# A slot more for streamed expert weights, and another order of the first expert group

## The chip, the cores and the metric

The kernel runs on 1 core of one Trainium2 chip. A time is the device time of one execution in microseconds (us). Before the change the median of 3 runs is 1218.99 us (1218.17 to 1219.28).

## The reference, cut to what matters

One decoder layer on 256 tokens of width 1024, all in float32. First a token mixer (modulated RMSNorm, one combined projection, gated linear attention and a short convolution, output projection), then a mixture of experts with 64 experts in 8 groups, of which each token uses 2:

```python
x = x + g1[:, None] * y                                   # after the mixer
h = rmsnorm(x, norm2_g[l]) * (1.0 + sc2[:, None]) + sh2[:, None]
p_group = softmax(t @ rg_w + rg_b); g_w, g_idx = top_k(p_group, 1)
e_w, e_loc = top_k(softmax(e_logits[of that group]), 2)   # weights then scaled by g_w
yb = (silu(xblk @ w1[e]) * (xblk @ w3[e])) @ w2[e]        # per expert, 1024 -> 512 -> 1024
x = x + g2[:, None] * y                                   # y: weighted sum of a token's two experts
out = rmsnorm(x, final_norm_g)
```

Every expert's w1, w3 and w2 (6 MB) is read once: 64 experts are 403 MB of the 476 MB that the kernel reads.

## The kernel before

**Stages.** The mixer runs over 88 blocks of projection weights (512 KB each, numbered 0 to 87; the last eight, 80 to 87, are the output projection `O0`, `O1`). TensorE works block after block, each in three passes with a weight split into a high and a low part (ACT line 320, DVE line 327). Then comes the router, then the experts in 16 groups of 4 (`EPG`). An expert group has room for 32 tokens of each of its experts (`CAP`), and 12 units of weights of 2 MB each: units 0 to 7 (`KT`) hold w1 and w3 by rows of the model width, units 8 to 11 hold w2. A token beyond an expert's 32 goes to overflow blocks, worked under a runtime condition before group 13 (`OVG`).

**A group's work.** `slots` writes on DVE the one-hot matrices `P1` and their sum `Pm` (which token goes where), `gather` multiplies the normalized residual with `Pm` on TensorE (line 994) and modulates the result into `xg` on ACT and DVE (lines 998, 1000), `slot_weights` scales `P1` by the router's weights (DVE, lines 1009, 1010) and transposes it on TensorE (line 1014). `l1_unit` multiplies with a unit of w1, w3 (line 1022), `act` does silu and product and transposes, `l2_unit` multiplies with w2, `evac_y` applies the gate, and `combine` brings the rows back to their tokens (line 1049) and adds them to the residual `acc` (line 1050). Within group g, `combine(g - 1)` comes after unit 2 and the inputs of group g + 1 after unit 4. In group 0 it is otherwise: its own gather stands between units 0 to 3, after unit 3 `after_start` (the router's weights and then the overflow tables, DVE lines 949 to 972), after unit 5 `after_start2` (`slot_weights(0)`, and the gate's row `g2r`, line 1075), after unit 6 the inputs of group 1.

**The stream of weights.** All loads of weights are issued by SyncE (SP) in program order, whenever the buffer of an earlier block or unit has been used: `Stream.bfree` (line 58, and line 66 where the blocks have run out) for a quarter of the ring, `Stream.free` (line 87) for a whole slot. There are ten slots of 2 MB: the ring of 12 blocks becomes three of them, the tiles T10, T11, T3, T9, T7, T6 and T4 of the mixer become the other seven, each when its last reader is done. So group 0's units 0 to 9 lie in T10, ring, T11, ring, T3, ring, T9, T7, T6, T4. Units 10 and up follow into whichever slot comes free; nothing but free buffers and the order of the program times them.

**Buffers that the change touches.** `xt` (tile T5) has four quarters of 4 KB per partition: 0 and 1 hold the transposed residual `xres`, later the two gather buffers `xg`; 2 and 3 are scratch of the mixer and then of the router (`r8`), later `y` and `g2r`. Tile T8 holds in turn several arrays of the mixer, at last `sg`, read by the evacuation of block 79; from `o_setup` (called ahead of block 82) it is `wk`: half 0 is the residual `acc`, half 1 its normalized copy `h2`, made by ACT at line 894 and read by every gather.

```python
S.activation(h2[:, tt], acc[:, tt], AF.Copy, scale=rs[:, tt:tt + 1])
...
            if u == (4 if g else 6) and g + 1 < NGRP and g + 1 != OVG:
```

Of the kernel before, what the change touches and what calls it, by code (L numbers as in the profile page):

```python
# [12 lines left out]
AF = mybir.ActivationFunctionType  # L13
# [6 lines left out]
TT = 2  # L20
# [20 lines left out]
CB, CN1, CN2, CGG, CCW, CGB, NCOL = 0, 48, 56, 64, 72, 96, 100  # L41


class Stream:


# [25 lines left out]
        self.bfree(self.at.pop(key))  # L72

    def slot(self, tag):
        if isinstance(tag, int):
            return self.ring[:, 4 * tag:4 * tag + 4].rearrange("p a b -> p (a b)")
        return self.pool.tile([128, 4096], F32, name="unit", tag=tag)

    def free(self, tag):
        if self.n == len(self.units):  # L80
            return
        key, pieces = self.units[self.n]
        self.n += 1
        t = self.slot(tag)
        self.tiles[key], self.tags[key] = t, tag
        for dst, src in pieces:
            self.nc.sync.dma_start(dst(t), src)

    def done(self, key, keep=False):
        tag = self.tags.pop(key)  # L90
        del self.tiles[key]
        if not keep:
            self.free(tag)
        return tag

# [2 lines left out]
def trunk_kernel(ctx: ExitStack, tc: tile.TileContext, xT: bass.AP, c: bass.AP, modw: bass.AP,  # L98
# [536 lines left out]
    B2 = modc[:, 24:32]  # L635
    rconst = sm.tile([128, 72], F32, name="rconst")
    ssq = sm.tile([128, TT, 5], F32, name="ssq")
    r8 = xt[:, 2:4].rearrange("p a b -> p (a b)")

    def pre_router():  # L640
        V.scalar_tensor_tensor(A2, modc[:, 32:40], 1.0, colt[:, CN2:CN2 + 8], op0=OP.add, op1=OP.mult)
# [133 lines left out]

    def o_setup():
        wk = big.tile([128, 2, TT, D], F32, name="wk", tag="T8")
        L["acc"], L["h2"] = wk[:, 0], wk[:, 1]
        L["pl"] = mt(2, 128)
        mring.remove((rot["m"] - 1) % 4)  # L780
        rot["m"] = 0
# [52 lines left out]
    evac(nb, *pend)  # L834
    run(nb)
    run(nb + 1)
    acc, h2 = L["acc"], L["h2"]
    assert not todo

    rs = sm.tile([128, 4], F32, name="rs")  # L840
# [6 lines left out]
    def scratch(*shape):  # L847
        n = 1
        for d in shape:
            n *= d  # L850
        t = r8[:, o[0]:o[0] + n]
        o[0] += n
        assert o[0] <= 2048
        if len(shape) == 2:
            t = t.rearrange("p (a b) -> p a b", a=shape[0])
        return t
# [4 lines left out]
    em, ei = scratch(2, 8), scratch(2, 8).bitcast(U32)  # L861
    OO = sm.tile([128, 2, 2, 64], BF, name="OO")
    O1, O2 = OO[:, :, 0], OO[:, :, 1]
    prr = scratch(4, 64).rearrange("p (t k) e -> p t k e", t=2)
    pr = prr.rearrange("p t k e -> p (t k e)")[:, 0:128].rearrange("p (t e) -> p t e", t=2)
    big8 = scratch(2, 2)
    nm, ex, zz, pw = scratch(2, 2), scratch(64), scratch(2, 2), scratch(2, 2)
# [23 lines left out]
    for tt in range(TT):  # L891
        V.max_index(gi[:, tt], gm[:, tt], lg[:, tt, :8])
    for tt in range(TT):
        S.activation(h2[:, tt], acc[:, tt], AF.Copy, scale=rs[:, tt:tt + 1])
    V.tensor_tensor(off8, io[:, None, :8].to_broadcast([128, 2, 8]), gi[:, :, 0:1].to_broadcast([128, 2, 8]),
                    op=OP.not_equal)
    V.scalar_tensor_tensor(lm.rearrange("p t (g e) -> p t g e", g=8), off8[:, :, :, None].to_broadcast([128, 2, 8, 8]),
# [50 lines left out]
    def overflow_tables():  # L948
        V.tensor_scalar(xb, cnt, float(CAP), None, op0=OP.is_gt)
        for m in range(2, 8):  # L950
            V.scalar_tensor_tensor(xb, cnt, float(CAP * m), xb, op0=OP.is_gt, op1=OP.add)
        V.tensor_tensor_scan(incl, onesf[:, :64], xb, 0.0, op0=OP.mult, op1=OP.add)
        V.tensor_sub(excl, incl, xb)
        for k, ot in enumerate((O1, O2)):
            for tt in range(TT):
                V.scalar_tensor_tensor(pr[:, tt], excl, 1.0, ot[:, tt], op0=OP.mult, op1=OP.mult,
                                       accum_out=ovs[:, tt, k:k + 1])
        V.scalar_tensor_tensor(dov, ovs, float(CAP), rank, op0=OP.mult, op1=OP.add)
        V.tensor_scalar(big8, rank, float(CAP), 8192.0, op0=OP.is_lt, op1=OP.mult)
        V.scalar_tensor_tensor(dov, dov, -float(CAP), big8, op0=OP.add, op1=OP.add)  # L960
        V.tensor_sub(dgo, dov.rearrange("p t k -> p (t k)")[:, :, None].to_broadcast([128, 4, 4]),
                     iog[:, None, 0:4].to_broadcast([128, 4, 4]))
        cmp = gt2[:, 0:NOV * 64].rearrange("p (b e) -> p b e", b=NOV)
        V.tensor_tensor(cmp, incl[:, None, :].to_broadcast([128, NOV, 64]),
                        io[:, :NOV, None].to_broadcast([128, NOV, 64]), op=OP.is_le)
        V.memset(ebi, 0)
        ef = fl(pr)[:, 0:NOV]
        V.tensor_reduce(ef, cmp, axis=AX.X, op=OP.add)
        V.tensor_scalar(ebi[:, 0, :NOV], ef, float(NE - 1), None, op0=OP.min)
        V.tensor_scalar(ebi[:, 1, :NOV], ebi[:, 0, :NOV], 2, None, op0=OP.arith_shift_right)  # L970
        V.tensor_scalar(ebi[:, 2, :NOV], ebi[:, 0, :NOV], 3, None, op0=OP.bitwise_and)
        V.tensor_copy(ebi[:, 0, 15:16], incl[:, 63:64])
# [12 lines left out]
    def gather_part(xg, i, split=False):  # L985
        if split:
            ps = [mt(128) for _ in range(2)]
        else:
            both = mt(2, 128)
            ps = [both[:, j] for j in range(2)]  # L990
        for j in range(2):
            for tt in range(TT):
                f = 256 * i + 128 * j
                T.matmul(ps[j], h2[:, tt, f:f + 128], Pm[:, tt], start=(tt == 0), stop=(tt == 1))  # L994
        for j in range(2):
            k = 2 * i + j
            if i % 2 == 0:
                S.activation(xg[:, k], ps[j], AF.Identity, bias=B2[:, k:k + 1], scale=A2[:, k:k + 1])  # L998
            else:
                V.tensor_scalar(xg[:, k], ps[j], A2[:, k:k + 1], B2[:, k:k + 1], op0=OP.mult, op1=OP.add)  # L1000
# [41 lines left out]
    def combine(key, c0=0, c1=D):  # L1042
        pwt = X["w", key]
        for c in range(c0, c1, 512):
            w = min(512, c1 - c)
            s = slice(c, c + w)
            for tt in range(TT):
                ps = mt()
                T.matmul(ps[:, :w], pwt[:, tt], X["y"][:, s], start=True, stop=True)  # L1049
                V.tensor_add(acc[:, tt, s], acc[:, tt, s], ps[:, :w])  # L1050

    V.tensor_tensor(Pm.rearrange("p t (j s) -> p t j s", j=EPG), pc[:, 0:2, 0:EPG, None].to_broadcast([128, TT, EPG, CAP]),
                    iof[:, None, None, :].to_broadcast([128, TT, EPG, CAP]), op=OP.is_equal)
# [5 lines left out]
    def after_start():  # L1059
        V.tensor_sub(dg, dst.rearrange("p t k -> p (t k)")[:, :, None].to_broadcast([128, 4, NGRP]),  # L1060
                     iog[:, None, 0:NGRP].to_broadcast([128, 4, NGRP]))
        for k in range(2):
            for tt in range(TT):
                V.tensor_scalar(P1[:, k, tt], io, dst[:, tt, k:k + 1], None, op0=OP.is_equal)
        weights()
        overflow_tables()
        S.activation(dum, epsc, AF.Silu)

    def after_start2():
        slot_weights(0)  # L1070
        for hh in range(2):
            p = mt(4, 128)
            for k in range(4):
# [36 lines left out]
                    combine("o")  # L1110

    OVG = NGRP - 3
    fgr = h2[:, 0]
    sq = h2[:, 1]

    def final_gain():
        for hh in range(2):
            p = mt()
            T.matmul(p, onesf[0:1, :], sq[0:1, 512 * hh:512 * hh + 512], start=True, stop=True)
            S.copy(fgr[:, 512 * hh:512 * hh + 512], p)  # L1120

    for g in range(NGRP):
        if g == OVG:
            combine(g - 1)
            held = st.done(("e", g - 1, NU - 1), keep=True)
            overflow(held)
            slots(g, dg, g)
            gather(g, g)
            slot_weights(g)
            st.free(held)  # L1130
        ps = pa.tile([128, D], F32, name="a")
        for u in range(KT):
            if g == 0 and u < 4:
                gather_part(X[0], u, u == 0)
            if g == last and u == 0:
                S.dma_start(sq[0:1, :], bass.AP(tensor=fg.tensor, offset=fg.offset, ap=[[D, 1], [1, D]]))
            if g == last and u == 5:
                final_gain()
# [1 line left out]
            st.done(("e", g, u))  # L1140
            if g == 0 and u == 3:
                after_start()
            if g == 0 and u == 5:
                after_start2()
            if u == 2 and g > 0 and g != OVG:
                combine(g - 1)
            if u == (4 if g else 6) and g + 1 < NGRP and g + 1 != OVG:
                slots(g + 1, dg, g + 1)
                gather(g + 1, g + 1)
                slot_weights(g + 1)  # L1150
        act(ps)
        ps = pa.tile([128, D], F32, name="a")
        if g < last:
            for f in range(4):
                l2_unit(ps, f, unit("e", g, KT + f))
                if not (g + 1 == OVG and f == 3):
                    st.done(("e", g, KT + f))
            evac_y(ps)
    S.activation(dum, epsc, AF.Sqrt)

# [6 lines left out]
    def last_part(n, tail=False):  # L1167
# [2 lines left out]
        evac_y(ps, c0, c0 + cw)  # L1170
        combine(last, c0, c0 + cw)
        for tt in range(TT):
            a = acc[:, tt, c0:c0 + cw]
            if tail and tt == 1:
                V.scalar_tensor_tensor(sq[:, c0:c0 + cw], a, 1.0, a, op0=OP.mult, op1=OP.mult,
                                       accum_out=ssq[:, tt, n:n + 1])
# [2 lines left out]

    def last_weigh(n):  # L1180
        c0, cw = LASTC[n]
        V.tensor_mul(acc[:, :, c0:c0 + cw], acc[:, :, c0:c0 + cw], fgr[:, None, c0:c0 + cw].to_broadcast([128, TT, cw]))  # L1182

    for u in range(2):
        w = st.tiles["e", last, KT + u].rearrange("p (f j c) -> p f j c", f=2, j=EPG)
# [21 lines left out]
    last_weigh(3)  # L1207
    V.reciprocal(rs[:, 0:2], rs[:, 0:2])
    lo, hi = slice(0, 512), slice(512, D)
    V.tensor_scalar(acc[:, 0, lo], acc[:, 0, lo], rs[:, 0:1], None, op0=OP.mult)  # L1210
    nc.sync.dma_start(out[0:128, lo], acc[:, 0, lo])
    S.activation(acc[:, 1, lo], acc[:, 1, lo], AF.Copy, scale=rs[:, 1:2])
    S.dma_start(out[128:256, lo], acc[:, 1, lo])
    for tt in range(TT):
        V.tensor_scalar(acc[:, tt, hi], acc[:, tt, hi], rs[:, tt:tt + 1], None, op0=OP.mult)
        nc.sync.dma_start(out[128 * tt:128 * tt + 128, hi], acc[:, tt, hi])


_INS = ["xT", "c", "modw", "cols", "win", "wgd", "gw2", "wr", "rb", "fg", "ew", "el"]
# [65 lines left out]
```

## Time and profile before

| what | value |
|---|---|
| median of 3 runs | 1218.99 us |
| the profiled execution's own time | 1218.99 us |
| its span, first to last instruction | 1216.9 us |
| bytes read from HBM | 475.79 MB |
| mean rate over the span | 393 GB/s |
| busy share PE / DVE / ACT | 74% / 31% / 18% |
| mean granted TensorE clock | 0.895 of full |

The span is cut into windows in which each engine's busy time, the granted clock (1.00 is 2.4 GHz, 0.50 is 1.2 GHz), the mean busy share of the 16 DMA engines and the rate of the transfers are given. SP's line in a timeline is the issue of a transfer; its bytes move later.

### The profile page before, as it was taken

How to read it: one execution, taken by the hardware profiler on the slowest of the kernel's cores; microseconds unless marked ns; L12 is line 12 of the kernel's file. 1: busy time of each engine (PE TensorE's matmuls, PEld its weight loads, DVE VectorE, ACT ScalarE, POOL GpSimd, SP SyncE). 2: the span in 40 equal slices, each digit the busy share in tenths (PEclk: the TensorE clock that was granted, in tenths of full speed). 3: DMA queues.
4: the chain of work that ended last, by engine and by line, in shares of the span. 5: the costliest groups of instructions: out<-in, count | busy, mean ns of one | idle time of the engine just before them, and what ended most of it. 6: DMA issues, size and time to landing. Idle time of an engine off the chain costs nothing. (4 is left out here: it accounts for less than half of the span.)

```text
span 1216.9 us, 14623 instructions
## 1 busy us (share of the span) xinstructions
PE 905.3 (74%) x6202; PEld 479.9 (39%) x6202; DVE 377.7 (31%) x716; ACT 224.8 (18%) x375; POOL 3.9 (0%) x15
## 2 busy tenths in 40 slices
PE   9999999999787656575766666665757655767565
PEld 6999999998323212121212121211212111412112
DVE  8967699664421202020202011111102010302003
ACT  6774455434201001010101010100000000100002
POOL 0000000000000000000000000000000000000000
PEclk9999999999889979788979788988888888988888
DMA  9987579978999999999999999999999999999995
GB/s 370 399 330 247 184 230 355 357 269 307 421 386 429 430 430 430 431 431 431 430 430 431 430 431 431 431 430 430 430 430 431 431 431 431 428 430 431 431 428 232
DMA packets 51337, 477.84 MB, mean 393 GB/s; under 512 B 5954, under 2 KB 6082, under 8 KB 27076
## 3 DMA queue, kind: packets, MB, share of 16 engines
q1 hardware_dynamic: 50400, 475.81, 94.7%
q10 hardware_dynamic: 868, 1.05, 0.2%
q8 instruction: 50, 0.82, 0.2%
q14 instruction: 19, 0.16, 0.0%
HBM read 475.79 MB, written 1.05 MB: 392 GB/s over the span
## 5 line engine op out<-in xcount | busy, mean ns | idle before, releaser
L1022 PE MATMUL a<-unit,xt 128*32 128x512 f32 x1424 | 206.2, 710 | 104.1 <-DMA unit<-in_ew_dram 104.1
L1022 PE MATMUL a<-unit,gt 128*32 128x512 f32 x672 | 112.6, 805 | 62.6 <-DMA unit<-in_ew_dram 58.1
L1022 PEld LDWEIGHTS a<-unit,xt 128*32 128x32 f32 x1424 | 44.7, 121 | 254.1 <-DMA unit<-in_ew_dram 131.7
L336 PE MATMUL z<-hhl,sp 128*128 128x256 f32 x1152 | 140.9, 284 | 0.0
L336 PEld LDWEIGHTS z<-hhl,sp 128*128 128x128 f32 x1152 | 138.9, 192 | 1.6 <-issue 1.5
L998 ACT ACTIVATE xt<-m,modc,A 128x128 f32<-128x128 f32 x64 | 25.9, 453 | 539.5 <-PE m L994 539.5
L327 DVE TENSOR_TENSOR sp<-ring,sp 128x1024 fp32r<-128x1024 f32 x88 | 106.9, 1221 | 42.6 <-ACT sp L320 40.9
L1022 PE MATMUL a<-ring,xt 128*32 128x512 f32 x624 | 85.6, 671 | 36.4 <-DMA ring<-in_ew_dram 36.4
L320 ACT CAST sp<-ring 128x1024 fp32r<-128x1024 f32 x88 | 91.5, 1048 | 96.0 <-PE z L336 64.8
L1050 DVE TENSOR_TENSOR wk<-wk,m 128x512 f32<-128x512 f32 (+2 forms) x68 | 44.5, 656 | 204.3 <-PE m L1049 204.2
L1040 DVE TENSOR_TENSOR xt<-a,xt 128x1024 f32<-128x1024 f32 (+3 forms) x19 | 20.0, 1055 | 272.0 <-PE a L1022 265.2
L1022 PEld LDWEIGHTS a<-unit,gt 128*32 128x32 f32 x672 | 22.3, 129 | 136.7 <-DMA unit<-in_ew_dram 81.5
L1022 PE MATMUL a<-ring,gt 128*32 128x512 f32 x288 | 48.1, 801 | 30.4 <-DMA ring<-in_ew_dram 30.4
L994 PEld LDWEIGHTS m<-Pm,wk 128*128 128x128 f32 x512 | 60.2, 196 | 22.1 <-issue 21.8
L994 PE MATMUL m<-Pm,wk 128*128 128x128 f32 x512 | 64.0, 283 | 6.0 <-DVE Pm L983 5.2
L1049 PE MATMUL m<-xt,pwt 128*128 128x512 f32 (+2 forms) x136 | 63.3, 608 | 5.3 <-DVE xt L1040 5.3
L1030 DVE TENSOR_TENSOR gt<-gt,a 128x512 f32<-128x512 f32 x16 | 11.0, 687 | 167.5 <-ACT gt L1029 167.5
L237 DVE SCALAR_TENSOR_TENSOR xt<-ring,xt 128x1024 f32<-128x1024 f32 x48 | 58.6, 1221 | 0.3
L1000 DVE TENSOR_SCALAR xt<-m,A,modc 128x128 f32<-128x128 f32 x64 | 23.3, 406 | 106.5 <-PE m L994 106.5
L1022 PEld LDWEIGHTS a<-ring,xt 128*32 128x32 f32 x624 | 17.4, 114 | 92.1 <-DMA ring<-in_ew_dram 58.5
L1049 PEld LDWEIGHTS m<-xt,pwt 128*128 128x128 f32 x136 | 25.5, 202 | 49.2 <-issue 36.6
L1029 ACT ACTIVATE gt<-a 128x512 f32<-128x512 f32 x16 | 9.6, 597 | 175.6 <-PE a L1022 175.6
(247 smaller groups left out, 628.4 us busy)
## 6 DMA issues: line engine op xcount, KB each, us to landing
unit<-in_ew_dram SPq DMA_DIRECT2D x131, 2048.0 KB, 38.8
ring<-in_ew_dram SPq DMA_DIRECT2D x54, 2048.0 KB, 38.8
ring<-in_win_dram SPq DMA_DIRECT2D x88, 512.0 KB, 8.0
ring<-in_modw_dram SPq DMA_DIRECT2D x48, 512.0 KB, 6.8
ring<-in_ew_dram SPq DMA_DIRECT2D x12, 512.0 KB, 6.2
unit<-in_el_dram SPq DMA_DIRECT2D x4, 1024.0 KB, 34.1
unit<-in_el_dram SPq DMA_DIRECT2D x4, 512.0 KB, 18.4
ring<-in_el_dram SPq DMA_DIRECT2D x4, 512.0 KB, 12.3
```

Source lines behind the costliest of these rows:

```text
L237: V.scalar_tensor_tensor(scr, st.block("m", i, b), 1.0, cB, op0=OP.mult, op1=OP.mult, accum_out=modc[:, 4 * i + b:4 * i + b + 1])
L320: S.copy(sp(b)[:, 0], st.block("w", n, i))
L327: V.tensor_sub(t[:, 1], st.block("w", n, i), t[:, 0].bitcast(F32))
L336: T.matmul(ps, t[:, ws, k], rhs[rs][:, k], start=(clear and k == 0 and n == 0), stop=(k == KT - 1 and n == 2), skip_group_check=True)
L994: T.matmul(ps[j], h2[:, tt, f:f + 128], Pm[:, tt], start=(tt == 0), stop=(tt == 1))
L998: S.activation(xg[:, k], ps[j], AF.Identity, bias=B2[:, k:k + 1], scale=A2[:, k:k + 1])
L1000: V.tensor_scalar(xg[:, k], ps[j], A2[:, k:k + 1], B2[:, k:k + 1], op0=OP.mult, op1=OP.add)
L1022: T.matmul(ps[32 * j:32 * j + 32, 512 * hh:512 * hh + 512], lhsT[:, 32 * j:32 * j + 32], w[:, j, 512 * hh:512 * hh + 512], start=first, st ...
L1030: V.tensor_mul(gt, gt, ps[:, 512:1024])
L1040: V.tensor_mul(X["y"][:, c0:c1], ps[:, c0:c1], X["g2r"][:, c0:c1])
L1049: T.matmul(ps[:, :w], pwt[:, tt], X["y"][:, s], start=True, stop=True)
L1050: V.tensor_add(acc[:, tt, s], acc[:, tt, s], ps[:, :w])
```

## The change

An eleventh place for one unit is made of the upper two quarters of `xt` and the upper half of `wk` (1 MB each, class `Halves`); it is loaded by two transfers, freed for loading in `o_setup`, and not loaded again after its use. To leave it free until then, the residual is normalized in place in `acc`; the router's scratch moves to `xt`'s quarter 1 (and `scr2`), the overflow tables' comparison from `gt2` to `xt`'s quarter 0; the experts' results are summed in `total` (the upper half of `wk`, written first by `combine(0)`), and in the last group `total` gets `acc` times the root mean square `std` added. In group 0 the units 4 to 7 follow each other; the overflow tables come behind `act`, `slot_weights(0)` and the gate's row behind the second unit of w2, the inputs of group 1 behind the fourth.

```diff
+class Halves:
+    def __init__(self, *parts):
+        self.parts = parts
+    ...
+    def __getitem__(self, i):
+        return self.view[i[1] // 2][:, i[1] % 2, i[2]]
 ...
@@ Stream.free
+        if isinstance(t, Halves):
+            for i, p in enumerate(t.parts):
+                self.nc.sync.dma_start(p, pieces[0][1][:, 2048 * i:2048 * i + 2048])
+            return
@@ Stream.done
-        if not keep:
+        if not keep and not isinstance(tag, Halves):
 ...
-    r8 = xt[:, 2:4].rearrange("p a b -> p (a b)")
+    r8 = xt[:, 1]
 ...
@@ o_setup
-        L["acc"], L["h2"] = wk[:, 0], wk[:, 1]
+        L["acc"], L["sum"] = wk[:, 0], wk[:, 1]
+        st.free(Halves(xt[:, 2:4].rearrange("p a b -> p (a b)"), wk[:, 1].rearrange("p a b -> p (a b)")))
 ...
-        S.activation(h2[:, tt], acc[:, tt], AF.Copy, scale=rs[:, tt:tt + 1])
+        S.activation(acc[:, tt], acc[:, tt], AF.Copy, scale=rs[:, tt:tt + 1])
 ...
-        cmp = gt2[:, 0:NOV * 64].rearrange("p (b e) -> p b e", b=NOV)
+        cmp = xt[:, 0, 0:NOV * 64].rearrange("p (b e) -> p b e", b=NOV)
 ...
@@ combine
-                V.tensor_add(acc[:, tt, s], acc[:, tt, s], ps[:, :w])
+                if key == 0:
+                    V.tensor_copy(total[:, tt, s], ps[:, :w])
+                else:
+                    V.tensor_add(total[:, tt, s], total[:, tt, s], ps[:, :w])
 ...
@@ after_start
-        overflow_tables()
 ...
@@ the loop over groups
             if g == last and u == 0:
+                for tt in range(TT):
+                    V.scalar_tensor_tensor(total[:, tt], acc[:, tt], std[:, tt:tt + 1], total[:, tt],
+                                           op0=OP.mult, op1=OP.add)
 ...
-            if g == 0 and u == 5:
-                after_start2()
-            if u == (4 if g else 6) and g + 1 < NGRP and g + 1 != OVG:
+            if u == 4 and 0 < g < last and g + 1 != OVG:
+                next_inputs(g + 1)
         act(ps)
+        if g == 0:
+            overflow_tables()
 ...
                 l2_unit(ps, f, unit("e", g, KT + f))
+                if g == 0 and f == 1:
+                    slot_weights(0)
+                    gate2_rows()
 ...
+            if g == 0:
+                next_inputs(1)
             evac_y(ps)
```

`next_inputs(g)` is `slots(g, dg, g)`, `gather(g, g)`, `slot_weights(g)`. The last group's norm and output read `total` in place of `acc`; its gain row and squares lie in `acc`'s two halves, which were `h2`'s.

## Rows read from the trace of the kernel before

**Rows 1.** The page's slices: transfer rate in 40 equal parts of the span
```profile
GB/s 370 399 330 247 184 230 355 357 269 307 421 386 429 430 430 430 431 431 431 430 430 431 430 431 431 431 430 430 430 430 431 431 431 431 428 430 431 431 428 232
```
**Rows 2.** The chain that ended last, from 1140 us: start, us, what
```profile
1146.78 38.84 DMA unit<-in_ew_dram
1185.67 3.60 PE a L1022 x16
```
**Rows 3.** Windows: PE, PEld, DVE, ACT, POOL busy, PEclk, DMA share, GB/s
```profile
210.00:220.00 10.00, 10.00 (x85) 10.00 (x85) 8.33 (x12) 5.01 (x6) 0.00 (x0) 1.00 1.03 420
280.00:292.00 12.00, 12.00 (x103) 12.00 (x103) 3.82 (x6) 3.42 (x9) 0.00 (x0) 1.00 0.81 283
292.00:296.00 4.00, 4.00 (x37) 4.00 (x36) 0.48 (x1) 1.43 (x5) 0.00 (x0) 1.00 0.94 397
296.00:300.00 4.00, 3.95 (x24) 2.88 (x24) 2.52 (x15) 1.47 (x8) 0.00 (x0) 1.00 0.69 213
...
310.00:342.00 32.00, 22.34 (x154) 10.23 (x152) 14.11 (x61) 10.04 (x24) 0.00 (x0) 0.80 1.01 429
342.00:356.00 14.00, 12.41 (x88) 3.72 (x92) 1.91 (x2) 0.73 (x2) 0.00 (x0) 0.73 0.91 335
360.00:1150.00 790.00, 518.73 (x3283) 165.54 (x3281) 118.14 (x266) 44.33 (x98) 0.00 (x0) 0.86 1.01 430
```
**Rows 4.** SP's issues from 279 us on: start, us, line, what is loaded
```profile
279.19 0.33 SPq L66 DMA_DIRECT2D ring<-in_ew_dram  x1
...
289.81 0.33 SPq L87 DMA_DIRECT2D unit<-in_ew_dram  x1
...
296.84 0.81 SPq L87 DMA_DIRECT2D unit<-in_ew_dram  x2
...
306.62 0.33 SPq L87 DMA_DIRECT2D unit<-in_ew_dram  x1
...
318.88 0.33 SPq L87 DMA_DIRECT2D ring<-in_ew_dram  x1
...
341.54 0.33 SPq L87 DMA_DIRECT2D unit<-in_ew_dram  x1
```
**Rows 5.** SP's waits, 240 to 360 us, by total, the first
```profile
SPq L87 <- PE a L1022: 55.9, 15, 13.3
```
**Rows 6.** SP's waits, 360 to 1180 us (total us, times, longest)
```profile
SPq L87 <- DMA unit<-in_ew_dram: 485.0, 110, 4.5
```
**Rows 7.** The page's DMA issues: what, count, KB each, median us from issue to landing
```profile
unit<-in_ew_dram SPq DMA_DIRECT2D x131, 2048.0 KB, 38.8
...
ring<-in_ew_dram SPq DMA_DIRECT2D x12, 512.0 KB, 6.2
```
**Rows 8.** Timeline of the last reads of `sg`: start, us, engine, line, operation
```profile
272.08 0.69 DVE L550 TENSOR_TENSOR yhl<-sg,yhl 128x512 fp32r<-128x512 f32 x1 [0.69 <-ACT yhl L547]
```
**Rows 9.** Timeline of group 0, 316 to 352 us
```profile
316.92 1.90 PE L1022 MATMUL a<-ring,xt 128*32 128x512 f32 x16
...
317.63 0.18 DVE L940 RECIPROCAL xt<-xt 128x4 f32<-128x4 f32 x1 [2.27 <-ACT xt L938]
...
319.02 0.19 DVE L949 TENSOR_SCALAR xt<-xt 128x64 f32<-128x64 f32 x1
...
326.19 1.06 PE L1014 MATMUL m<-ident,P 128*128 128x128 f32 x2 [7.36 <-DVE P L1010]
...
328.88 3.64 PE L1022 MATMUL a<-unit,xt 128*32 128x512 f32 x16
...
332.45 3.84 PE L994 MATMUL m<-Pm,wk 128*128 128x128 f32 x32
...
341.55 0.60 ACT L1029 ACTIVATE gt<-a 128x512 f32<-128x512 f32 x1 [2.53 <-PE a L1022]
...
344.71 7.72 PE L1022 MATMUL a<-unit,gt 128*32 128x512 f32 x48 [0.67 <-ACT gt L1034]
```
**Rows 10.** The page's groups: the mixer's scalar_tensor_tensor over 128x1024
```profile
L237 DVE SCALAR_TENSOR_TENSOR xt<-ring,xt 128x1024 f32<-128x1024 f32 x48 | 58.6, 1221 | 0.3
```

More of the change, by code (lines that the diff above doesn't have):

```diff
@@ L41, with rearrange @@
 CB, CN1, CN2, CGG, CCW, CGB, NCOL = 0, 48, 56, 64, 72, 96, 100
+class Halves:
+    def __init__(self, *parts):
+        self.parts = parts
+    def rearrange(self, *a, b):
+        self.view = [p.rearrange("p (b k) -> p b k", b=b // 2) for p in self.parts]
+        return self
+    def __getitem__(self, i):
+        return self.view[i[1] // 2][:, i[1] % 2, i[2]]
 class Stream:
@@ L74, in slot @@
     def slot(self, tag):
+        if isinstance(tag, Halves):
+            return tag
         if isinstance(tag, int):
@@ L836, in trunk_kernel @@
     run(nb + 1)
-    acc, h2 = L["acc"], L["h2"]
+    acc, total = L["acc"], L["sum"]
     assert not todo
@@ L852, in scratch @@
         o[0] += n
-        assert o[0] <= 2048
+        assert o[0] <= 1024
         if len(shape) == 2:
@@ L863, in trunk_kernel @@
     O1, O2 = OO[:, :, 0], OO[:, :, 1]
-    prr = scratch(4, 64).rearrange("p (t k) e -> p t k e", t=2)
+    prr = scr2.rearrange("p (t k e) -> p t k e", t=2, k=2)
     pr = prr.rearrange("p t k e -> p (t k e)")[:, 0:128].rearrange("p (t e) -> p t e", t=2)
@@ L993, in gather_part @@
                 f = 256 * i + 128 * j
-                T.matmul(ps[j], h2[:, tt, f:f + 128], Pm[:, tt], start=(tt == 0), stop=(tt == 1))
+                T.matmul(ps[j], acc[:, tt, f:f + 128], Pm[:, tt], start=(tt == 0), stop=(tt == 1))
         for j in range(2):
@@ L1065, in after_start, with gate2_rows @@
         weights()
-        overflow_tables()
         S.activation(dum, epsc, AF.Silu)
-    def after_start2():
-        slot_weights(0)
+    def gate2_rows():
         for hh in range(2):
@@ L1112, in trunk_kernel @@
     OVG = NGRP - 3
-    fgr = h2[:, 0]
-    sq = h2[:, 1]
+    fgr = acc[:, 0]
+    sq = acc[:, 1]
     def final_gain():
@@ L1120, in final_gain, with next_inputs @@
             S.copy(fgr[:, 512 * hh:512 * hh + 512], p)
+    def next_inputs(g):
+        slots(g, dg, g)
+        gather(g, g)
+        slot_weights(g)
     for g in range(NGRP):
@@ L1126, in trunk_kernel @@
             overflow(held)
-            slots(g, dg, g)
-            gather(g, g)
-            slot_weights(g)
+            next_inputs(g)
             st.free(held)
@@ L1142, in trunk_kernel @@
                 after_start()
-            if g == 0 and u == 5:
-                after_start2()
             if u == 2 and g > 0 and g != OVG:
                 combine(g - 1)
-            if u == (4 if g else 6) and g + 1 < NGRP and g + 1 != OVG:
-                slots(g + 1, dg, g + 1)
-                gather(g + 1, g + 1)
-                slot_weights(g + 1)
+            if u == 4 and 0 < g < last and g + 1 != OVG:
+                next_inputs(g + 1)
         act(ps)
+        if g == 0:
+            overflow_tables()
         ps = pa.tile([128, D], F32, name="a")
@@ L1172, in last_part @@
         for tt in range(TT):
-            a = acc[:, tt, c0:c0 + cw]
+            a = total[:, tt, c0:c0 + cw]
             if tail and tt == 1:
@@ L1181, in last_weigh @@
         c0, cw = LASTC[n]
-        V.tensor_mul(acc[:, :, c0:c0 + cw], acc[:, :, c0:c0 + cw], fgr[:, None, c0:c0 + cw].to_broadcast([128, TT, cw]))
+        V.tensor_mul(total[:, :, c0:c0 + cw], total[:, :, c0:c0 + cw], fgr[:, None, c0:c0 + cw].to_broadcast([128, TT, cw]))
     for u in range(2):
@@ L1209, in trunk_kernel @@
     lo, hi = slice(0, 512), slice(512, D)
[L1210 to L1213, printed above, removed]
+    V.tensor_scalar(total[:, 0, lo], total[:, 0, lo], rs[:, 0:1], None, op0=OP.mult)
+    nc.sync.dma_start(out[0:128, lo], total[:, 0, lo])
+    S.activation(total[:, 1, lo], total[:, 1, lo], AF.Copy, scale=rs[:, 1:2])
+    S.dma_start(out[128:256, lo], total[:, 1, lo])
     for tt in range(TT):
-        V.tensor_scalar(acc[:, tt, hi], acc[:, tt, hi], rs[:, tt:tt + 1], None, op0=OP.mult)
-        nc.sync.dma_start(out[128 * tt:128 * tt + 128, hi], acc[:, tt, hi])
+        V.tensor_scalar(total[:, tt, hi], total[:, tt, hi], rs[:, tt:tt + 1], None, op0=OP.mult)
+        nc.sync.dma_start(out[128 * tt:128 * tt + 128, hi], total[:, tt, hi])
 _INS = ["xT", "c", "modw", "cols", "win", "wgd", "gw2", "wr", "rb", "fg", "ew", "el"]
```

## The prediction
> **What bounds the kernel now.** Three views, in this order. First the slices of the page: the reader is to see that the rate swings between 184 and 421 GB/s in the first twelve and then stands at 428 to 431 until the last one [rows 1]. Next the chain of waits: its end is a transfer of weights that lands at 1185.6 us, then TensorE's work on it and a tail to the span's end [rows 2]. So from 360 us on the stream of weights is the kernel; the window from 360 to 1150 us gives its full rate, 430 GB/s, with PE busy for 519 of 790 us [rows 3]. A unit of 2.097 MB takes 2.097/0.430 = 4.88 us of it. The bytes are fixed, so only time in which the stream runs below 430 ahead of that can be won, and I measure it in bytes.
>
> Third, the windows of that earlier time. From 280 to 292 us the rate is 283, which leaves out (430-283)*12 = 1.76 MB; from 292 to 296 0.13 MB and from 296 to 300 0.87 MB; from 310 to 342 it is full at 429; from 342 to 356 us (430-335)*14 = 1.33 MB are left out [rows 3]. The issues say why. Around 280 us the blocks are used up and no slot is free: after a quarter of the ring at 279.19 come two more quarters, T7 only at 289.81, T6 and T4 at 296.84, T10 again at 306.62 [rows 4]. Around 342 us the used units come too slowly: unit 5 is given back at 318.88, unit 7 only at 341.54, and the longest of SP's waits on TensorE between 240 and 360 us is 13.3 us [rows 4, 5].
>
> Does an eleventh slot help after that? No: from 360 us SP waits mostly for an earlier transfer (485 us in 110 waits), and a unit lands 38.8 us after its issue, which is 38.8/4.88 = 8 units under way [rows 6, 7]. Ten slots already hold more than these. Its whole worth is one unit loaded in the hole.
>
> **The slot.** SP issues its two halves behind block 85's quarter (279.19) and ahead of block 86's; each issue takes 0.33 us, so the quarter behind still finds its turn near 281 us. The halves wait for the last reader of `sg`, done at 272.8 [rows 8], and for the mixer's scratch, done long before; so they wait for nothing. Before, the queue had run empty ahead of T7's issue. Now 2.10 MB lie in a hole of 1.76 MB; the 0.33 MB that are over push T7's bytes by 0.8 us into the hole of 0.87 MB behind them. All fits: **4.88 us** earlier, in whole. Bounds: 0, if it is issued after 289.8; 4.88, as a unit can't save more than its own time. The unit in it is number 7, read at about 321 us, far behind its landing at about 289.
>
> At 512 KB a transfer, 210 to 220 us, the full queue moves 420 GB/s [rows 3]; against 430 that is 0.524/0.420-0.524/0.430 = 0.03 us a transfer, my value for the second half's start. The other end is a quarter's 6.2 us to landing less its 1.2 of moving, 5.0 us [rows 7]; the row with the full queue is the near one. The Trainium skill speaks against cutting a load in two: "DMA: Bandwidth & Descriptors", section "Anatomy of one DMA", charges each transfer (on the GpSimd path) some 2.0 us besides its bytes. By that the second half costs 2.0 us more and the sum would be 1213.0.
>
> **Group 0's order.** Through unit 5 nothing changes on TensorE (ends 318.8) [rows 9]. What stood behind it goes: the overflow tables, begun at 319.02, for which TensorE sat 7.36 us up to 326.19; the scale and gate's transposes up to 328.88; a unit at half clock, 3.64 us (PEclk fell while it sat); the inputs of group 1 from 332.45 to 338.5 [rows 9]. Units 6 and 7 now follow at 1.9 us each: 322.6. `act` takes 344.71-341.55 = 3.2 us: 325.8. Two units of w2: 329.6. The tables (from 319.02 to TensorE's release at 326.19 they and `slot_weights`' scaling take DVE 7.2 us) run from about 324.5 to 331.7 beside them; there `slot_weights(0)` has a wait: TensorE stands some 2 us, with the gate's transposes, two units of w2 and group 1's gather queued behind, and after them SP's returns. With 1 and 2 us for the transposes, units 10 and 11 end near 338.5, group 1's inputs (6.1 us, as before) at about 345, its first unit at 347.
>
> Is the stream fed through that? T6 and T4, issued at 296.84, flow from about 298.5 and end 9.8 us later, at 308.3. Behind it stand units 0 to 6 given back by 321 (7's place is not): 7*4.88 = 34.2 us, to 342.5. Units 8 and 9 come by 330: to 352. Units 10, 11 by 338.5: to 362. Group 1's first at 347. Never empty: the missing 1.33 MB go, **3.09 us**. At half clock w2's units take 3.64 instead of 1.9: 8 and 9 back at 333, 10 and 11 at 344, group 1's first at about 356, still ahead of 342.5, 352 and 362. This reserve of 6 us and more hides the tables' new place, the DVE wait and all of `next_inputs(1)`; without it each us of TensorE's delay costs a us. Bounds of this part: 0 and 3.09.
>
> **What costs nothing.** Normalizing in place, the copy instead of the first addition and the moved scratch have the same instructions. New are two DVE operations in the last group, 2*1.22 = 2.44 us by the nearest row [rows 10]; ACT's load of the gain row waits for them, behind it only `act`, 30 us later; the group lasts 12*4.88 = 58.6 us and DVE is 31% busy. POOL's queue is untouched. If the cover failed, 2.44 us.
>
> **Sum.** 4.88+3.09 = 7.97 us. The profiled execution took 1218.99 us, span 1216.9 and 2.1 around it, which is also the median. 1218.99-7.97 = 1211.0 us. Its own range is 1209.0 to 1213.0: the last unit of w1, w3 took 3.60 us [rows 2] where 1.90 is full speed [rows 9], so the tail may shift by about 1.7 us either way.
>
> **The rivals.** (1) Slot yes, order no: DVE's tables hold the chain so long that the stream still empties. For it: 7.36 us of that wait stand in the trace [rows 9]; against it the reserve above. 1218.99-4.88 = 1214.1.
> (2) Order yes, slot no: the halves are held until T7's time. 1218.99-3.09 = 1215.9.
> (3) Slower. SP issues in order; if the halves wait for whole tiles, `xt` is in use until the logits of block 87, which I put 1.4 us behind T6's issue [rows 4], at 298.2, and the quarters of blocks 86 and 87, T7 and T6 stand behind them. The stream then lacks 1.05+2.10 MB and about 0.3 MB of T6 at 300, 3.45 MB or 8.0 us; less 3.09 that is 4.9 later: 1223.9. It decides once SP is held to about 292.5 us, where the loss (1.05 MB and T7's first 1.15) equals the 0.87 and 1.33 MB of holes that the then full queue closes. Against it: DVE writes scratch in `xt` at 317.63 while TensorE reads another quarter of it from 316.92 to 318.8 [rows 9], so parts of a tile are told apart.
> (4) Neither does what it says: what SP waits for is an earlier transfer, as later in the run, and a free slot is no use. For it the later waits [rows 6]; against it the early ones, where TensorE leads [rows 5]. 1219.0.
> (5) The second half pays its start in full, 5.0 us: 1216.0. Only a queue run empty would show it, and T9's and the ring's bytes are moving then.
>
> **Chances.** The forecast 0.74, (1) 0.07, (2) 0.06, (3) 0.05, (4) 0.03, (5) 0.03, a larger gain by a faster tail 0.02. The range 1208.8 to 1214.3 holds nearly all of the forecast's own cases and (1), and leaves out the rest. This kernel's runs tell 0.2% (2.4 us) from no change: faster 0.92 (forecast, 1, 2, 5, tail), same 0.03, slower 0.05.
>
> The skill's same page, section "Bandwidth", has the HBM side bind at about 358 GB/s for a core. By that a unit is worth 5.86 us and the second hole (358-335)*14 = 0.32 MB, 0.9 us: 1212.2. The trace disagrees, 430 held over 790 us [rows 3].
>
> **What would show it.** After: two issues of 1 MB between 279.2 and 281; a rate near 430 from 281 to 296 and no window under 400 between 300 and 360; PE L1022 unbroken from unit 4 to unit 7; the tables behind `act`; the transfer that ends the chain landing about 8 us sooner. Wrong if the halves' issue stands behind 285 us, if the stream dips again near 340 to 360, or if the tail behind the last landing grows.

## The result, and the profile after

The changed kernel took 1210.64 us (median of 4 runs, 1209.19 to 1211.79), the kernel before beside it 1218.58 (4 runs, 1217.48 to 1219.28): ratio 0.9944 [0.9929, 0.9959], by the ratio 6.8 us less (5.0 to 8.7), by the medians 7.9. The forecast was 1211.0. The profiled execution took 1211.79, span 1210.0. Below, "the start of the last unit" is that of TensorE's work on unit 7 of the last group. It begins as that unit's transfer lands. Only that group's w2 (8 MB, `in_el_dram`) lands later. So this start dates the end of the stream of units, "the stream's end", apart from what follows, "the tail".

The chain of waits, its end, in the kernel after (start, us, what), against [rows 2]:

```profile
1143.26 33.98 DMA unit<-in_ew_dram
1177.28 2.94 PE a L1043 x16
```

1185.67 became 1177.28: the stream ends 8.39 us sooner (forecast 7.97). From there to the span's end it is 32.7 us, before 31.2, so 1.5 us are lost again in the tail (more on it at the end of the account).

The windows (columns as in [rows 3]), kernel after:

```profile
280.00:292.00 12.00, 12.00 (x103) 12.00 (x103) 3.60 (x6) 3.19 (x9) 0.00 (x0) 1.00 0.99 406
292.00:296.00 4.00, 4.00 (x37) 4.00 (x36) 0.48 (x1) 1.43 (x5) 0.00 (x0) 1.00 1.03 422
296.00:300.00 4.00, 3.95 (x22) 2.77 (x22) 2.74 (x17) 1.69 (x8) 0.00 (x0) 1.00 0.89 307
308.00:312.00 4.00, 4.00 (x37) 1.51 (x28) 0.21 (x1) 1.56 (x3) 0.00 (x0) 1.00 0.90 328
310.00:342.00 32.00, 27.52 (x224) 11.71 (x226) 15.17 (x63) 10.31 (x25) 0.00 (x0) 0.94 1.00 420
342.00:356.00 14.00, 14.00 (x88) 3.90 (x88) 4.68 (x10) 0.37 (x1) 0.00 (x0) 0.88 1.01 432
360.00:1150.00 790.00, 524.19 (x3240) 161.51 (x3244) 115.80 (x257) 42.77 (x94) 0.00 (x0) 0.84 1.01 431
```

The hole from 280 to 300 shrank from 2.76 MB to (430-406)*12 + 8*4 + 123*4 = 0.81 MB; the dip from 342 to 356 (1.33 MB) is gone. One at 308 to 312 has deepened to (430-328)*4 = 0.41 MB; before it was 0.23:

```profile
308.00:312.00 4.00, 4.00 (x40) 1.65 (x32) 0.42 (x2) 1.35 (x3) 0.00 (x0) 1.00 0.97 373
```

From 360 us on all is as before.

SP's issues in the kernel after (columns as in [rows 4]):

```profile
279.35 0.43 SPq L104 DMA_DIRECT2D xt<-in_ew_dram  x1
279.83 0.44 SPq L104 DMA_DIRECT2D wk<-in_ew_dram  x1
280.65 0.33 SPq L80 DMA_DIRECT2D ring<-in_ew_dram  x1
289.58 0.33 SPq L107 DMA_DIRECT2D unit<-in_ew_dram  x1
296.62 1.58 SPq L107 DMA_DIRECT2D unit<-in_ew_dram  x2
306.41 0.33 SPq L107 DMA_DIRECT2D unit<-in_ew_dram  x1
```

The halves go out at once, and the quarter behind them finds its turn at 280.65. SP's longest wait on TensorE between 240 and 360 us, against [rows 5]:

```profile
SPq L107 <- PE a L1043: 51.8, 16, 9.2
```

The timeline of group 0 after (start, us, engine, line, operation, idle before), against [rows 9]:

```profile
318.43 1.90 PE L1043 MATMUL a<-unit,xt 128*32 128x512 f32 x16
...
323.35 0.19 DVE L970 TENSOR_SCALAR xt<-xt 128x64 f32<-128x64 f32 x1
...
324.81 5.28 PE L1043 MATMUL a<-unit,gt 128*32 128x512 f32 x32 [0.67 <-ACT gt L1055]
...
330.51 0.33 PE L1035 MATMUL m<-ident,P 128*128 128x128 f32 x1 [0.42 <-DVE P L1031]
...
332.23 3.64 PE L1043 MATMUL a<-unit,gt 128*32 128x512 f32 x32
335.80 3.84 PE L1015 MATMUL m<-Pm,wk 128*128 128x128 f32 x32
...
341.89 3.56 PE L1043 MATMUL a<-ring,xt 128*32 128x512 f32 x16
```

Unit 6 starts at 318.43, about where the tables stood before; they begin at 323.35 (forecast 324.5). The wait for DVE that I put at 2 us is 0.42 here, because one of the two units of w2 ahead of it ran at half clock; in the runs in which both took 3.64 us together it is 2.05 or 2.06 (order only, the changed kernel beside the held clock). Units 10 and 11 end at 335.9 (forecast 338.5), group 1's first unit at 345.5 (347). One unit of w2 and group 1's first ran at half clock, 3.56 us for the latter; the stream did not notice.

### The profile page after: what moved, and what is told of

Its sections match the earlier page's. It is cut to its first block, busy times and chain, and to the rows that moved or that the text cites. A ratio compares the mean times of both kernels' runs of the same rounds, so it can differ in the third digit from the quotient of the medians.

```text
span 1210.0 us, 14630 instructions
## 1 busy us (share of the span) xinstructions
PE 912.2 (75%) x6202; PEld 478.8 (40%) x6202; DVE 380.1 (31%) x718; ACT 224.7 (19%) x375; POOL 4.0 (0%) x15
## 4 chain that ended last, share of the span: by engine, by line
DMA 67%; PE 29%; DVE 3%; ACT 0%; issue 0%; DVEq 0%; SPq 0%; ACTq 0%
DMA ring<-in_ew_dram 39%; DMA unit<-in_ew_dram 28%; PE z L356 17%; PE a L1043 3%; PE m L364 2%; PE z L373 2%; PE m L1015 1%; PE m L1070 1%; PE a L1195 1%; PE m L529 0%; PE z L220 0%; PE m L506 0%; PE m L525 0%; PE m L296 0%; PE m L312 0%
## 5 line engine op out<-in xcount | busy, mean ns | idle before, releaser
L1043 PE MATMUL a<-unit,xt 128*32 128x512 f32 x1408 | 202.0, 703 | 92.4 <-DMA unit<-in_ew_dram 92.4
L1043 PE MATMUL a<-ring,xt 128*32 128x512 f32 x624 | 92.3, 718 | 45.9 <-DMA ring<-in_ew_dram 45.9
L1074 DVE TENSOR_TENSOR wk<-wk,m 128x512 f32<-128x512 f32 (+2 forms) x64 | 41.8, 655 | 196.3 <-PE m L1070 196.3
L1043 PE MATMUL a<-ring,gt 128*32 128x512 f32 x288 | 51.0, 842 | 22.2 <-DMA ring<-in_ew_dram 20.0
L1015 PEld LDWEIGHTS m<-Pm,wk 128*128 128x128 f32 x512 | 58.7, 192 | 19.0 <-issue 18.7
L1043 PEld LDWEIGHTS a<-ring,xt 128*32 128x32 f32 x624 | 20.1, 123 | 115.3 <-DMA ring<-in_ew_dram 59.9
## 6 DMA issues: line engine op xcount, KB each, us to landing
unit<-in_ew_dram SPq DMA_DIRECT2D x130, 2048.0 KB, 38.8
ring<-in_ew_dram SPq DMA_DIRECT2D x54, 2048.0 KB, 38.8
```

Of the source, the lines that this page charges most:

```text
L1015: T.matmul(ps[j], acc[:, tt, f:f + 128], Pm[:, tt], start=(tt == 0), stop=(tt == 1))
L1043: T.matmul(ps[32 * j:32 * j + 32, 512 * hh:512 * hh + 512], lhsT[:, 32 * j:32 * j + 32], w[:, j, 512 * hh:512 * hh + 512], start=first, st ...
L1074: V.tensor_add(total[:, tt, s], total[:, tt, s], ps[:, :w])
```

## The experiments

Each ran against the kernel before on the same chip. Gains below are by the ratio; those by the medians differ by up to 1.5 us. Single profiles stand up to 1.3 us apart before any of the changed stages: TensorE begins the same matmul of the router between 301.5 and 302.8 us. The last column is free of that. It counts the bytes of SP's transfers in the trace: the time from the arrival of the 85th MB (at 282 to 283 us) to that of the 140th.

| kernel | last unit starts, us | from there to the span's end | 85th to 140th MB, us |
|---|---|---|---|
| before, first profile | 1185.67 | 31.2 | 138.7 |
| before, once more | 1181.81 | 30.4 | 135.7 |
| after, three profiles | 1177.28, 1177.64, 1176.96 | 32.7, 31.4, 31.3 | 131.3, 131.3, 131.3 |
| slot only | 1182.71 | 30.2 | 136.5 |
| order only | 1182.47 | 30.3 | 135.8 |
| late slot | 1179.93 | 33.2 | 135.0 |
| after, clock held in the last group | 1177.13 | 34.0 | 130.9 |
| before, clock held in the wait | 1181.72 | 30.4 | 136.1 |

**Slot only: group 0 in the old order.**

```diff
@@ after_start
+        overflow_tables()
@@ the loop over groups
+            if g == 0 and u == 5:
+                slot_weights(0)
-            if u == 4 and 0 < g < last and g + 1 != OVG:
+            if u == (4 if g else 6) and g < last and g + 1 != OVG:
 ...
-        act(ps)
         if g == 0:
-            overflow_tables()
+            gate2_rows()
+        act(ps)
 ...
```

> The eleventh slot with group 0 in the old order (tables in after_start, slot_weights(0) after unit 5, group 1's inputs after unit 6; only the gate's row, whose place the slot takes, is written after unit 7). Theory A, the prediction's two terms added up: the slot is worth its 4.88 us by itself, 1218.6 - 4.9 = 1213.7, and a dip between 342 and 356 us as before. Theory B, the terms hang together: unit 7's place is not given back, so in the old order, where the stream runs dry at 342 us anyway, one give-back less comes before it; from 342.5 to about 350 nothing moves, some 4.3 us more than before, and of the slot's 4.88 us about 0.5 are left: 1218.

1215.33 (12 runs) against 1216.42 (33): 0.9979 [0.9966, 0.9992]. Its windows:

```profile
280.00:292.00 12.00, 12.00 (x103) 12.00 (x103) 4.20 (x6) 3.77 (x11) 0.00 (x0) 1.00 0.99 407
342.00:356.00 14.00, 12.26 (x103) 3.55 (x106) 1.91 (x2) 0.87 (x2) 0.00 (x0) 0.88 0.67 262
```

The hole is filled as in the whole change, but the dip is deeper: (430-262)*14 = 2.35 MB against 1.33, 2.4 us more. Of 4.88 us 2.5 are left by the windows of these two profiles, and 2.2 by the table's last column. The time fell by 2.6 (1.0 to 4.1; by the medians 1.1), which agrees loosely. The deeper dip rests on this one profile, of 1214.78 us; two of the twelve runs took 1212.1 and 1212.3, and whether they had it was not seen. The slot is not loaded again, so unit 7's use gives nothing back, and in the old order the next place after unit 6's comes from unit 8. SP's issues show it:

```profile
331.26 0.33 SPq L107 DMA_DIRECT2D unit<-in_ew_dram  x1
347.65 2.04 SPq L107 DMA_DIRECT2D unit<-in_ew_dram  x2
```

**Order only: the place is not made.**

```diff
-        st.free(Halves(xt[:, 2:4].rearrange("p a b -> p (a b)"), wk[:, 1].rearrange("p a b -> p (a b)")))
```

> Group 0's new order and all else of the change, but the halves are never freed for loading: ten slots as before. Prediction's second term: the dip from 342 to 356 us goes, the hole from 280 to 292 stays: 1218.6 - 3.1 = 1215.5. Rival, the order is worth nothing without the slot: 1218.6.

1214.75 (12 runs): 0.9985 [0.9973, 0.9997], 1.8 us less. Its windows:

```profile
280.00:292.00 12.00, 12.00 (x105) 12.00 (x104) 4.20 (x6) 4.08 (x12) 0.00 (x0) 1.00 0.80 292
342.00:356.00 14.00, 13.77 (x96) 4.83 (x97) 5.55 (x12) 0.37 (x1) 0.00 (x0) 1.00 1.01 431
```

The hole is back, the dip gone. Against the first profile of before the stream ends 3.2 us sooner, as its bytes say (3.09), but against the second 0.7 us later; the median gains less. That gap is taken up below.

**Late slot: the place is made behind T4's.** (Here the gate's row is written over a part of unit 10, so group 0's results differ; the amount of work is the same.)

```diff
@@ o_setup
-        st.free(Halves(...))
+        L["halves"] = Halves(...)
@@ behind the last block
     st.free("T4")
+    st.free(L["halves"])
```

> The halves are freed last of all, behind T7, T6 and T4 (about 298 us instead of 279.5). Theory, the slot is worth the hole that it fills: the hole from 282 to 291 us comes back, and the unit's bytes come behind T4's, where they fill only the small dip at 308 to 312 us (about 1 us): 3.9 us longer than the changed kernel, 1214.5. Rival, only the number of units that fit ahead of group 0's first give-back counts, not when they are loaded: 1210.6.

1214.33 (10 runs): 0.9972 [0.9960, 0.9984]; the stream ends 2.6 us later than in the first profile of after. Its windows:

```profile
280.00:292.00 12.00, 12.00 (x104) 12.00 (x103) 3.26 (x6) 2.85 (x7) 0.00 (x0) 1.00 0.77 275
296.00:300.00 4.00, 3.95 (x21) 2.62 (x20) 3.01 (x19) 2.03 (x8) 0.00 (x0) 1.00 0.66 209
308.00:312.00 4.00, 4.00 (x37) 1.60 (x30) 0.00 (x0) 1.91 (x3) 0.00 (x0) 1.00 1.01 426
```

What counts is being early: issued some 17 us later the slot loses most of its worth. Against order only it keeps 0.8 us by the table's last column. That is what fits into the window from 308 to 312, which is full here; the hole from 280 to 300 is as empty as without the slot (209 GB/s from 296 on). The measured times alone don't tell so much: late slot and order only lie 0.4 us apart by the medians, 1.6 by the ratios.

**Two transfers for every unit.**

```diff
+        if len(pieces) == 1:
+            for i in range(2):
+                s = slice(2048 * i, 2048 * i + 2048)
+                self.nc.sync.dma_start(t[:, s], pieces[0][1][:, s])
+            return
```

> Every unit of 2 MB that came in one transfer comes in two of 1 MB (some 184 transfers more). Theory 1, a transfer behind others costs about 0.03 us (the bound of the prediction): 184 * 0.03 = 5.5 us longer, 1216. Theory 2, nothing: 1210.6. Theory 3, the 2 us per transfer of the Trainium skill's page on DMA, in full: 368 us longer. And for what limits the transfers under way: if it is their number, 8, a transfer now lands 8 * 2.44 = 19.5 us after its issue; if it is bytes or slots, 38.8 us as before.

1218.22 (12 runs): 1.0017 [0.9997, 1.0038], against 0.9944 to 0.9960 for the changed kernel some 7 to 9 us, by 184 more transfers 0.04 to 0.05 us each. The window of full rate and the page's issues (as in [rows 7]):

```profile
360.00:1150.00 790.00, 562.20 (x3220) 173.50 (x3224) 114.73 (x257) 42.76 (x94) 0.00 (x0) 0.95 1.01 427
```

```profile
unit<-in_ew_dram SPq DMA_DIRECT2D x260, 1024.0 KB, 19.6
```

427 for 431 over 790 us is 7.3 us. At this price the split of one unit in the change costs next to nothing. The Trainium skill ("DMA: Bandwidth & Descriptors", section "Anatomy of one DMA") gives some 2 us a transfer on the GpSimd path, for 184 transfers an estimate of 368 us; on SP's full queue no run shows it.

**The changed kernel again, and TensorE made to stand.** Idle matmuls in the changed kernel ask how much delay the stream bears: 28 or 56 behind `act` of group 0, or 12 ahead of its gather.

```diff
+    def stand(n):
+        p = mt()
+        for _ in range(n):
+            T.matmul(p, ident, acc[:, 0, 0:512], start=True, stop=True)
 ...
         if g == 0:
+            stand(28)
             overflow_tables()
```

> The changed kernel once more, beside the three that follow and on their chip: 7.97 us less than the kernel before, a ratio of 0.9935, by the prediction's sum; 0.9929 to 0.9959 by its first runs.

> 28 matmuls of 128x512 (0.43 us each, some 12 us) that nothing reads are put on TensorE in group 0, behind act and ahead of the first unit of w2. Theory, the reserve: the stream is fed until about 343 us by units 0 to 6; the first unit of w2 is given back at about 338.6 instead of 326.6, still ahead of that: no change against the changed kernel (ratio to before 0.994, no window under 400 GB/s between 312 and 360 us). Rival, TensorE's time in group 0 is on the path: 12 us longer (1.004).

> The same with 56 matmuls, some 24 us. Theory: the first unit of w2 comes back at about 350.6, its bytes flow from 352.2, the stream is empty from 343.4: 8.8 us longer than the changed kernel (ratio to before about 1.0010), the empty stretch seen in the windows. Rival, all on the path: 24 us longer (1.014). Rival, all hidden: 0.994.

> 12 such matmuls (some 5.2 us) ahead of group 0's first gather, of which some 0.6 us lie in a wait. Theory: all slots are full and the stream runs empty at about 308 us, so the time of unit 0's give-back is on the path: 4.6 us longer than the changed kernel (ratio to before 0.998), the empty stretch behind 308 us. Rival, it is hidden like any other work of TensorE in group 0: 0.994.

Again: 1210.98 (5 runs), 0.9960 [0.9946, 0.9973]. The sizes were off: each matmul has two records of 0.43 us in the trace and takes 0.86, not half. In the timelines, of the run of 28, of that of 56 and of that of 12 ahead of group 0:

```profile
324.61 24.20 PE L1147 MATMUL m<-wk,ident 128*128 128x512 f32 x56
```

```profile
324.53 48.23 PE L1147 MATMUL m<-wk,ident 128*128 128x512 f32 x112
```

```profile
302.82 10.55 PE L1152 MATMUL m<-wk,ident 128*128 128x512 f32 x24
```

24.2 us of standing cost 1219.49 (6 runs) - 1210.98 = 8.5 us, 48.2 us cost 1244.06 (5 runs) - 1210.98 = 33.1. So 15.7 and 15.1 us are free, and every one behind them costs one. (Ratios to before: 1.0030 [1.0018, 1.0042] and 1.0231 [1.0217, 1.0245].) So the expectation for 24 us (8.8 us longer) came true with the 28 matmuls, and the one for 28 was a miss by their size alone. With 28 the dip is back, deeper:

```profile
342.00:356.00 14.00, 14.00 (x82) 5.47 (x84) 1.30 (x5) 1.45 (x3) 0.00 (x0) 1.00 0.45 166
```

Ahead of group 0 there is next to no reserve: 10.55 us cost 1218.74 (9 runs) - 1210.98 = 7.8 us (1.0027 [1.0017, 1.0037]). The gather, and with it unit 0's return of T10, came about 10 us later (306.41 to 316.35), and the queue, whose last load ahead of that is T4's, ran dry:

```profile
308.00:312.00 4.00, 4.00 (x11) 1.79 (x10) 0.00 (x0) 0.00 (x0) 0.00 (x0) 1.00 0.19 82
```

**The clock held in the last group, the changed kernel beside it, and before once more.**

```diff
             l1_unit(ps, g, u, unit("e", g, u))
+            if g == last and u > 2:
+                hold_clock(2 if u < 7 else 1)
```

`hold_clock` is so many idle matmuls of 128x512.

> The changed kernel with matmuls that nothing reads behind each of the last group's units 3 to 6 (two of 128x512, 1.7 us) and behind unit 7 (one), in TensorE's waits for the next unit. Theory: in the tail TensorE's clock is at half in part (the last unit of w1, w3 took 2.91 us in the changed kernel, 1.90 at full); where TensorE waits less between units, as in the run with two transfers a unit (granted clock 0.95 from 360 to 1150 us instead of 0.84), it stays up. The last unit then takes 1.9 us, the first 32 matmuls of w2 end with the landing of their second unit, and from unit 7's start to the span's end it is 31.0 us instead of 31.4 to 32.7: 0.5 to 1.5 us less than the changed kernel. Rival, the added matmuls delay the last units: 1 to 2 us more. Rival, the clock doesn't rise: same.

> The changed kernel beside it, for the comparison on one chip: a ratio to before of 0.993 to 0.997.

> One look at the kernel before on this chip: where do 1215.6 us here and 1218.6 us of the first runs differ? If it is the tail's clock: the last unit of w1, w3 starts at 1185.7 us as in the first profile, with a shorter way from there to the end than 31.2 us. If it is the stream: it starts earlier.

Held: 1212.86 (6 runs), 0.9957 [0.9942, 0.9973]; the changed kernel beside it 1211.00 (6 runs), 0.9948 [0.9934, 0.9961]. No gain, and by the medians 1.9 us longer, though the two intervals overlap. The last unit took 1.92 us (3.23 beside it), but the clock fell behind it, and the combine, 1.98 us elsewhere, ran at half:

```profile
1177.13 1.92 PE L1043 MATMUL a<-unit,xt 128*32 128x512 f32 x16 [0.20 <-DMA unit<-in_ew_dram]
...
1189.69 3.78 PE L1070 MATMUL m<-xt,pwt 128*128 128x512 f32 x4 [0.81 <-DVE xt L1061]
```

There was nothing to gain at that unit either. In the changed kernel beside it, where it took 3.23 us, the combine began 11.7 us behind its start, no later than in the changed kernel's second profile, where it took 1.92.

The second profile of before shows something else: 1214.22, and no dip.

```profile
330.00:332.00 2.00, 2.00 (x21) 0.83 (x14) 0.00 (x0) 0.01 (x1) 0.00 (x0) 1.00 1.01 430
...
340.00:342.00 2.00, 0.65 (x4) 0.42 (x4) 0.69 (x1) 0.53 (x2) 0.00 (x0) 1.00 0.96 410
...
342.00:356.00 14.00, 13.81 (x116) 4.41 (x117) 1.72 (x2) 0.14 (x1) 0.00 (x0) 1.00 1.01 431
```

The same windows in the first profile of before (335 GB/s from 342 to 356, [rows 3]):

```profile
330.00:332.00 2.00, 2.00 (x12) 0.19 (x4) 0.00 (x0) 0.00 (x0) 0.00 (x0) 0.50 0.99 426
...
340.00:342.00 2.00, 1.50 (x8) 0.00 (x0) 0.00 (x0) 0.45 (x1) 0.00 (x0) 0.50 0.99 426
```

In both the granted clock falls to 0.50 while TensorE waits for DVE's tables, from about 323 us on. In the new one it is back at 330 and unit 6 takes 2.17 us (timeline); in the first it is 0.50 over all of unit 6 (3.64) and again near 340, and the stream empties. The times of before point the same way: of its 77 runs beside the changed kernels 41 took less than 1217 us and 28 more than 1218, with 8 between, while the 15 runs of the changed kernel lie within 2.6 us. The first four of before, which the forecast and the first ratio rest on, are all above 1217.4.

**Before, with the clock held through that wait.**

```diff
     def after_start2():
+        p = mt()
+        for _ in range(8):
+            T.matmul(p, ident, h2[:, 0, 0:512], start=True, stop=True)
         slot_weights(0)
```

> The kernel before, with 8 matmuls of 128x512 that nothing reads (0.86 us each, 6.9 us) in TensorE's wait of 7.36 us in group 0, behind unit 5. Theory: the dip from 342 to 356 us is there only where TensorE's clock, fallen in that wait, stays at half over unit 6 and falls again near 340 (the first profile, unit 6 at 3.64 us); the second profile of the same kernel had unit 6 at 2.17 us and no dip. With the clock held unit 6 takes 1.9 us and the dip is gone in every execution: all runs in the lower of the two groups that the runs of the kernel before form (1214 to 1217 and 1218 to 1220 us), median 1215.2. Rival, the dip comes from the order and the wait alone: the same two groups, a ratio of 1.000 to before.

1214.39 (11 runs, 1213.34 to 1215.85) against 1218.24 (15 runs, 1214.88 to 1221.13): 0.9975 [0.9964, 0.9985], 3.0 us less by 7.13 us of added work. Unit 6 in its timeline, and the window:

```profile
327.90 1.92 PE L1022 MATMUL a<-unit,xt 128*32 128x512 f32 x16
```

```profile
342.00:356.00 14.00, 13.81 (x112) 3.87 (x112) 1.23 (x1) 0.14 (x1) 0.00 (x0) 0.88 1.00 417
```

Now the runs lie within 2.5 us, where those of before span 6.3; they lie at the fast end of before's. Unit 6 ends 2.7 us sooner than in the first profile ([rows 9]), though unit 7 then ran at half clock. The missing bytes, (430-417)*14 = 0.18 MB, are a seventh of the dip. No kernel tried beats the changed one.

## Why the prediction was right, step by step

**The stream as bound**: held. Span and stream's end move together, with a tail of 30.2 to 34.0 us behind it, and delays of TensorE cost nothing until the queue is empty.

**The slot, 4.88 us**: held, if not quite "in whole". By profiles without a dip on either side it is 4.4 to 4.8 us in the table's last column (135.7 to 136.1 against 131.3), and 4.1 to 5.5 by the start of the last unit. A part of the unit's worth is lost again in the window from 308 to 312. The halves were issued at the time said. Rivals 2 and 3 (halves held, SP held) are out by the issues of after, rival 4 (a free slot no use) by the bytes that now fill the hole, rival 5 (the second half's start) by the 406 GB/s in it and by 0.04 to 0.05 us a transfer.

**The order, 3.09 us**: right for the profile it was worked out from (138.7 us against 135.8 in order only, 2.9 us), mis-founded as a fixed term. The step that took the 1.33 MB as lost in every execution failed: the second profile of before has none. What empties the stream is the old order's wait together with a clock that stays down behind it; the run with the clock held confirms it. So the gain depends on which course before takes. By the medians it went from 4.6 us (1215.57 to 1210.98) over 6.4 (1217.44 to 1211.00) to 7.9 (1218.58 to 1210.64), while the changed kernel stays at 1210.6 to 1211.0. That the medians of before differ by their share of executions with a dip is argued, from two profiles and the spread of the runs. What decides for an execution whether the clock comes back early is open. That the full sum of 7.97 us came out is thus in part luck: it was set against runs that all lie at the slow end of before.

**The two terms as a sum**: they are not independent. The slot's unit gives no place back, so without the order the slot deepens the dip, by the windows. The times agree but don't decide it: alone the terms are worth 2.6 and 1.8 us, together 4.9 to 6.8, each known to some 1.5 us. Rival 1, the slot with a stream that still empties, was put at 1214.1 by the full 4.88 us; this leaves out the deeper dip, 2.4 us.

**The reserve, 6 us and more**: 15 us by both standing runs, and next to none ahead of unit 0's return. The prediction's balance counted places from unit 0 on and passed over that edge: T4's bytes end at 308.3 by its own working, and T10 is given back at 306.4. From 308 to 309 the rate falls to about 210 GB/s in the trace of after. The window at 308 to 312 stood in the trace of before (0.23 MB) inside a stretch read as full from 310 to 342, and it grew to 0.41 MB, about 1 us. The late slot fills it. The forecast's sign "no window under 400 between 300 and 360" failed there (328).

**The free edits**: the two operations in the last group took 2.47 us (2.44 said) and the stream's rate around them (1140 to 1150 us) did not fall, 435 GB/s for 429.

**The tail**: 1.5 us longer in the first profile, 0.1 to 1.0 by the others, within the 1.7 said; but that it must not grow was one of the prediction's signs. It has two parts, divided by the start of the last group's first combine, before and after:

```profile
1198.21 2.00 PE m L1049 x4
```

```profile
1190.31 2.00 PE m L1070 x4
```

Ahead of it TensorE's clock decides: 12.5 us before and 13.0 after with the last unit at half clock, 11.6 and 11.7 in the second profile of before and the other two of after, where the chain runs over the landing of w2's bytes instead (there one last unit of 3.23 us cost nothing). Behind it lies a loss that the sum does not have: 18.7 us before, 19.7 in all three profiles of after. At the end of after's transfers, from 1204 to 1211 us in 40 slices, some 0.01 MB follow behind the last store, by the profile a load of instructions, and the span ends 1.4 us behind them:

```profile
GB/s 0 0 0 0 0 140 410 410 410 387 375 421 410 433 410 386 363 398 433 421 164 0 12 23 23 12 0 0 0 0 0 0 0 0 0 0 0 0 0 0
```

Before, nothing follows the last store; in slot only and order only this load stands elsewhere, and the second part is 18.6 and 18.7 us. In all nine profiles that have the load there this part is 19.6 us or more. No run moved the load by itself, so that it is the cause is not shown.

## What to carry to other kernels

Balance a stream by time: when each buffer is given back against when the queue will run dry; an extra buffer is worth at most its own load, and only in a hole of the stream and only while enough others come back. Before a stall seen in one profile is credited as a gain, look at how far the runs of the kernel scatter and profile it a second time: the stall may stand in a part of the executions alone. And date the stream's end by the landing of one late load, the same in every run, apart from the tail.

## What the runs showed of the hardware

- With two transfers a unit the granted clock from 360 to 1150 us rose from 0.84 to 0.95 with the same work in it, though the kernel got slower: where the stream is the bound, a higher clock bought no time.
- Issue to landing halved with the transfer's size, 38.8 us at 2 MB and 19.6 at 1 MB: 8 under way either way (19.6/2.45). Whether the chip or the program sets this number no run shows.
- Idle matmuls that keep the clock up can pay where TensorE is not the bound: 7.13 us of them in a wait saved 3.0 us. In the last group they moved the fall onto the combine (3.78 us for 1.98) and gained nothing.
